# Merging triangle inverses with a transposed bracket: both factors read along a contiguous last index, three transposing copies on ScalarE per group

## The chip, the cores and the metric

One NeuronCore of a Trainium2 chip runs the whole program. The metric is device time in microseconds (us) of one execution; lower is better. The engines are called as the profile calls them: PE is TensorE (matmul), PEld its weight load, DVE is VectorE, ACT is ScalarE, POOL is GpSimd, and SP is SyncE, which here only issues DMAs.

## What is computed

The reference is a stack of two two-layer blocks in float32 on 256 tokens plus 256 context tokens. The change lies in the first layer, an RWKV-7 mixer: 32 heads of 64 channels, a recurrence over the tokens run forwards and backwards, and a readout with a normalisation per head:

```python
def step(s, inp):
    r_t, w_t, k_t, v_t, a_t, b_t = inp
    sa = jnp.einsum('bhvk,bhk->bhv', s, a_t)
    s = s * w_t[:, :, None, :] + sa[..., None] * b_t[:, :, None, :] + v_t[..., None] * k_t[:, :, None, :]
    return s, jnp.einsum('bhvk,bhk->bhv', s, r_t)
...
yn = merge_heads((y - mean) * lax.rsqrt(var + RWKV_GN_EPS))
yn = yn * p['ln_w'].astype(jnp.float32) + p['ln_b'].astype(jnp.float32)
return ((yn + merge_heads(bonus)) * jax.nn.silu(gate.astype(jnp.float32))).astype(dtype)
```

Inside a chunk of 64 tokens the term in `sa` couples every token with all earlier ones. The kernel solves that with the inverse of a triangular 64x64 matrix for each chunk, head and direction.

## The kernel before

**Stages.** After the projections of layer 0, the RWKV core works through eight groups of 256 channels (four heads each). Group g has four generators: `rwkv_prep` makes the scaled operands (AR, BK, PC), `rwkv_inverse` makes the inverses TT, `rwkv_chain` runs 16 steps (8 chunks in each of 2 directions), and `rwkv_readout` normalises and gates. `rwkv_core` (L765) interleaves them: while the chain of group g runs, the inverse of g+1, the prep of g+2 and the readout of g-1 are advanced between its steps, and so are the modulation vectors of later layers (`matvec`) and, in the last two groups, the filters of the next layer. Group 0's inverse runs earlier, beside the last projection (the gates, L702). After the core come the output product, a Hyena layer and the whole second block.

**The chain.** A step makes masked scores on PE into the PSUM tile `qk`, which DVE empties into `ATT` (L1052); then `ry` on PE, a copy to `RB` on ACT (L1083), `us` = TT times RB on PE (L1087), a copy to `UV` (L1088), the new state `st` on PE, a copy `St` on ACT (L1099), and the state update on POOL (L1101 adds, L1102 multiplies into `SB`), which the next step's `ry` of that direction reads. `qk` has two buffers, so PE stands when DVE is late with ATT.

**The inverse.** A transpose on DVE (L974) puts one 32x32 triangle on each of 128 partitions. `lane_inverse` (L1118) inverts it there. Seven small steps (L1134) invert the four 8x8 diagonal blocks. `merge8` (L1140) joins two 8x8 blocks to a 16x16 one, at rows 0 and at rows 16. `merge16` (L1154) joins those to 32x32. Each merge is two products: the bracket Z = A times X, with X the inverse of the upper block, and then the inverse of the lower block times Z. Every product is one elementwise multiply of two broadcast operands into `prod`, with index order (t, s, j) (L1131), and one sum over j (L1132). Each of merge16's two products is cut in three pieces. DVE multiplies two; POOL multiplies the third (into a tile `L`); DVE sums all three. In the layout before, the second factor is X or Z read through a rearrangement with j as its last index, so that neighbours in j lie 32, 8 or 16 floats apart. Then come two transposes (L984), copies to TT on ACT (L990), and small PE products that fill in the rest of the 64x64 inverse.

**The order.** The kernel is written against a tile framework that orders each engine's queue by playing the program through (L1917), so an edit in one place also moves other instructions. Each engine works its queue in order.

**The readout** (L1173) loads v, gate, `ln_w` (tile `rlw`) and `ln_b` (tile `rlb`) through SP's queue at its start. POOL multiplies by `rlw` (L1201) and adds `rlb` (L1202), between other steps.

## Time and profile before

| | |
|---|---|
| median of 3 runs | 2563.92 us (2564.22, 2563.92, 2555.0) |
| the profiled execution's own time | 2559.34 us |
| its span, first to last instruction | 2557.6 us |
| PE busy | 2366.6 us (93%) |
| DVE busy | 1508.1 us (59%) |
| ACT busy | 1232.6 us (48%) |
| POOL busy | 831.7 us (33%) |
[...]

The shares are averages over unlike stages, so a stage is read by itself: first how busy each engine is in it, then who ended PE's waits. A row of the views by shape gives a count, busy time in us, the mean of one in ns, the idle time before them and what ended it.

### The profile page before, as it was taken

The numbers are of one execution on the slowest core, as the hardware profiler recorded it, in microseconds if no ns is written. First come the engines' busy times: TensorE is split into PE (matmuls) and PEld (weight loads), VectorE is DVE, ScalarE is ACT, GpSimd is POOL, SyncE is SP. The second block draws the span as 40 slices with busy tenths as digits, with TensorE's granted clock in tenths as the row PEclk, the third lists the DMA queues.
The fourth block names the chain that finished last, engine by engine and source line by source line (L and its number), as shares of the span: only waits on it lengthen the run. The fifth ranks groups of instructions, "written<-read, shape, count | busy, mean of one in ns | idle before, by whom it ended". The sixth has DMA issues, their size and how long they took to land. (4 is left out here: it accounts for less than half of the span.)

```text
span 2557.6 us, 46534 instructions
## 1 busy us (share of the span) xinstructions
PE 2366.6 (93%) x19171; PEld 1992.6 (78%) x19171; DVE 1508.1 (59%) x2182; ACT 1232.6 (48%) x2270; POOL 831.7 (33%) x800
## 2 busy tenths in 40 slices
PE   6999989888887898989999999999999999999998
PEld 4578867666675676777779998788899987888886
DVE  6564495675858658665466666552435634654464
ACT  4345456665565665745344444432235623433453
POOL 4234344463545545442113332120022211121231
PEclk9999996988898988989999999999999999999999
DMA  6546442233232322204455554333222232434333
GB/s 218 201 132 204 158 141 69 85 100 107 83 113 85 120 89 79 82 21 158 149 171 173 166 169 158 115 99 99 66 85 84 65 109 83 129 124 133 108 124 132
DMA packets 203768, 306.01 MB, mean 120 GB/s; under 512 B 12593, under 2 KB 110542, under 8 KB 203556
## 3 DMA queue, kind: packets, MB, share of 16 engines
q1 hardware_dynamic: 194528, 276.08, 33.6%
q0 software_dynamic: 6096, 19.77, 2.1%
q10 hardware_dynamic: 2932, 7.18, 0.9%
q8 instruction: 151, 2.47, 0.4%
q14 instruction: 61, 0.50, 0.1%
HBM read 281.93 MB, written 21.06 MB: 118 GB/s over the span
## 5 line engine op out<-in xcount | busy, mean ns | idle before, releaser
L155 DVE TENSOR_TENSOR wlo<-wraw,whi 128x2048 fp32r<-128x2048 f32 (+1 forms) x156 | 364.5, 2338 | 310.8 <-ACT whi L154 310.6
L154 ACT CAST whi<-wraw 128x2048 fp32r<-128x2048 f32 (+1 forms) x172 | 321.9, 1875 | 296.4 <-PE x L151 153.4
L151 PE MATMUL mm<-whi,hH 128*128 128x256 f32 (+1 forms) x944 | 301.7, 322 | 4.5 <-DVE ropet L1518 1.9
L151 PE MATMUL mm<-wlo,hH 128*128 128x256 f32 (+1 forms) x944 | 300.7, 319 | 0.1
L151 PE MATMUL mm<-whi,hL 128*128 128x256 f32 (+1 forms) x944 | 299.9, 319 | 0.0
L151 PEld LDWEIGHTS mm<-whi,hH 128*128 128x128 f32 x944 | 178.5, 190 | 19.2 <-ACT rs_junk L399 2.0
L151 PEld LDWEIGHTS mm<-wlo,hH 128*128 128x128 f32 x944 | 179.0, 190 | 14.2 <-POOL wlo L155 0.3
L151 PEld LDWEIGHTS mm<-whi,hL 128*128 128x128 f32 x944 | 178.8, 190 | 14.0 <-DVE hL L355 0.2
L1052 DVE TENSOR_TENSOR ATT<-qk,mask 128x512 f32<-128x512 f32 (+1 forms) x128 | 70.6, 552 | 133.5 <-PE ry L151 86.9
L151 PE MATMUL x<-wlo,hH 128*128 128x512 f32 x352 | 140.9, 401 | 0.7 <-POOL wlo L155 0.7
L151 PE MATMUL x<-whi,hH 128*128 128x512 f32 x352 | 138.3, 399 | 1.9 <-ACT whi L154 1.9
L151 PE MATMUL ry<-UV,ATT 128*64 128x64 f32 x1536 | 139.8, 240 | 0.0
L151 PE MATMUL x<-whi,hL 128*128 128x512 f32 x352 | 139.6, 399 | 0.0
L155 POOL TENSOR_TENSOR wlo<-wraw,whi 128x2048 fp32r<-128x2048 f32 x16 | 73.6, 4598 | 201.2 <-ACT whi L154 201.2
L151 PEld LDWEIGHTS ry<-UV,ATT 128*64 128x64 f32 x1536 | 118.2, 150 | 22.2 <-issue 10.3
L1101 POOL TENSOR_TENSOR St<-St,SB 128x256 f32<-128x256 f32 x84 | 80.5, 960 | 139.0 <-ACT St L1099 131.7
L151 PE MATMUL qk<-PD,BKx 128*128 128x256 f32 x256 | 82.7, 453 | 22.4 <-DVE ATT L1052 20.9
L151 PE MATMUL us<-RB,TT 128*64 128x64 f32 x1024 | 91.1, 236 | 2.2 <-ACT RB L1083 2.0
L151 PEld LDWEIGHTS us<-RB,TT 128*64 128x64 f32 x1024 | 73.8, 145 | 21.6 <-issue 7.1
L1102 POOL TENSOR_TENSOR SB<-St,PC 128x256 f32<-128x256 f32 x98 | 81.6, 833 | 17.2 <-ACT St L1099 13.3
L1083 ACT COPY RB<-ry 64x256 f32<-64x256 f32 x128 | 46.7, 365 | 82.7 <-PE ry L151 81.0
L151 PE MATMUL us<-UV,BKt 128*128 128x128 f32 x448 | 80.5, 306 | 5.7 <-ACT UV L1088 5.6
(573 smaller groups left out, 6511.2 us busy)
## 6 DMA issues: line engine op xcount, KB each, us to landing
wraw<-in_w_in SPq DMA_DIRECT2D x68, 1024.0 KB
wraw<-in_l_w_in SPq DMA_DIRECT2D x64, 1024.0 KB
raw<-in_w_mod SPq DMA_DIRECT2D x48, 512.0 KB
wraw<-in_w_out SPq DMA_DIRECT2D x24, 1024.0 KB
raw<-in_ada_w SPq DMA_DIRECT2D x24, 512.0 KB
wraw<-in_w_branch_out SPq DMA_DIRECT2D x12, 1024.0 KB
UV<-vD SPq DMA_DIRECT2D x128, 64.0 KB
lH<-in_ada_w SPq DMA_DIRECT2D x5, 1024.0 KB
```

Of the source, the lines that this page charges most:

```text
L151: return self.nc.tensor.matmul(out, lhsT, rhs, start=start, stop=stop)
L154: self.nc.scalar.copy(hi, src)
L155: (eng or self.nc.vector).tensor_tensor(lo, src, hi.bitcast(F32), ALU.subtract)
L1052: nc.vector.tensor_tensor(at.rearrange("p i j a t -> p (i j) (a t)"), q[:, 0:256 * na].rearrange("p (h n) -> p h n", h=4), mk, ALU.mult)
L1083: nc.scalar.copy(rhs[zr], ry[0:64, 0:256])
L1101: nc.gpsimd.tensor_tensor(tmp, tmp, SB[z][step % 2], ALU.add)
L1102: nc.gpsimd.tensor_tensor(SB[z][1 - step % 2], tmp, pc, ALU.mult)
```

## The change

Four edits, three in `lane_inverse` and one in `rwkv_readout`.

1. A new tile `mW` (384 floats per partition) takes transposed copies of the upper blocks' inverses. Two copies of 8x8 (ACT, ahead of the merges) and one of 16x16 (ACT, behind `merge8(0)`) are made in each group.
2. The first product of each merge now has index order (s, t, j), from `mW` and A, so Z is stored transposed. The second product has (t, s, j) as before and reads Z as it lies. All factors have j as their contiguous last index.
3. The pieces, their sizes and their engines stay: per group four DVE multiplies of 512 elements, four of 1024, two POOL multiplies of 1024, and the same sums.
4. The readout's `ln_b` no longer has a tile of its own. It is loaded into tile `rlw` after the two multiplies by `ln_w`, and the two adds follow after a `yield`.

```diff
+        W = self.t(pool, [128, 384], "mW")
+        W8 = W[:, 0:128].rearrange("p (r a b) -> p r a b", r=2, b=8)
+        W16 = W[:, 128:384].rearrange("p (a b) -> p a b", b=16)
+        for r in range(2):
+            nc.scalar.copy(W8[:, r], X2[:, 16 * r:16 * r + 8, 16 * r:16 * r + 8].rearrange("p j s -> p s j"))
...
-            a = A2[:, r1:r1 + n, r0:r1].unsqueeze(2).to_broadcast([128, n, n, n])
-            xb = X2[:, r0:r1, r0:r1].rearrange("p s j -> p j s")
-            mulred(Z, a, xb.unsqueeze(1).to_broadcast([128, n, n, n]), (n, n, n))
+            a = A2[:, r1:r1 + n, r0:r1].unsqueeze(1).to_broadcast([128, n, n, n])
+            mulred(Z, W8[:, r0 // 16].unsqueeze(2).to_broadcast([128, n, n, n]), a, (n, n, n))
...
-            zb = Z.rearrange("p s j -> p j s")
-            mulred(X2[:, r1:r1 + n, r0:r1], a, zb.unsqueeze(1).to_broadcast([128, n, n, n]), (n, n, n))
+            mulred(X2[:, r1:r1 + n, r0:r1], a, Z.unsqueeze(1).to_broadcast([128, n, n, n]), (n, n, n))
...
+                    if n == 0:
+                        a, b = W16[:, s, j], A2[:, 16:32, 0:16][:, t, j]
+                        mulred(Z[:, s, t], a.unsqueeze(2).to_broadcast([128, ns, nt, nj]), b.unsqueeze(1).to_broadcast([128, ns, nt, nj]), (ns, nt, nj), eng)
+                    else:
+                        a, b = X2[:, 16:32, 16:32][:, t, j], Z[:, s, j]
+                        mulred(X2[:, 16:32, 0:16][:, t, s], a.unsqueeze(2).to_broadcast([128, nt, ns, nj]), b.unsqueeze(1).to_broadcast([128, nt, ns, nj]), (nt, ns, nj), eng)
...
         yield from merge8(0)
+        nc.scalar.copy(W16, X2[:, 0:16, 0:16].rearrange("p j s -> p s j"))
         yield from merge8(16)
...
-        lb = self.t(p1, [128, 256], "rlb")
-        nc.sync.dma_start(lb, I["l0_ln_b"][ch0:ch0 + 256].partition_broadcast(128))
...
             nc.gpsimd.tensor_tensor(Y[0][:, i], Y[0][:, i], lw, ALU.mult)
+        lb = self.t(p1, [128, 256], "rlw")
+        nc.sync.dma_start(lb, I["l0_ln_b"][ch0:ch0 + 256].partition_broadcast(128))
+        yield 1
+        for i in range(2):
             nc.gpsimd.tensor_tensor(Y[0][:, i], Y[0][:, i], lb, ALU.add)
-        yield 1
```

The queues differ from group 0's merges to the end of the core; ahead of that and from the output product on they read alike, but for a few rows.

DVE's queue in group 1, before, from the first bracket to the second (`prod` takes the products, `L` holds A and X, `mZ` is Z; kd, BKc, BKx and ARc belong to the prep, cols to the modulations):

```order
L1132 TENSOR_REDUCE L_3641<-prod_3714 128x4x7
L1131 TENSOR_TENSOR prod_3718<-L_3640,L_3641 128x512
L906 TENSOR_TENSOR kd_3592<-kd_3592,K_3571 128x512
L1132 TENSOR_REDUCE mZ_3717<-prod_3718 128x64
L918 TENSOR_TENSOR BKc_604_3561<-kd_3592,F_3586 128x4x64
L918 TENSOR_TENSOR BKx_605_3562<-kd_3592,F_3586 128x4x64
L923 TENSOR_TENSOR ARc_608_3565<-N_3575,P_3657 128x256
L1131 TENSOR_TENSOR prod_3772<-L_3641,mZ_3717 128x512
L1052 TENSOR_TENSOR ATT_3957<-qk_3958,mask_3278 128x512
```

The same place after the change (`mW` written by ACT):

```order
L1132 TENSOR_REDUCE L_3645<-prod_3718 128x4x7
L906 TENSOR_TENSOR kd_3596<-kd_3596,K_3575 128x512
L918 TENSOR_TENSOR BKc_605_3565<-kd_3596,F_3590 128x4x64
L918 TENSOR_TENSOR BKx_606_3566<-kd_3596,F_3590 128x4x64
L1131 TENSOR_TENSOR prod_3725<-mW_3721,L_3644 128x512
L315 TENSOR_REDUCE cols_31_133<-pp_3733 128x4
L1052 TENSOR_TENSOR ATT_3916<-qk_3917,mask_3282 128x512
```

The first bracket stood right behind the last small step; now three prep instructions lie between them, and an ATT stands close behind it.

POOL's queue at the first readout, before (`rrs` is its scale, `Y` its tile, `St` and `SB` are the chain's state):

```order
L163 TENSOR_TENSOR rrs_5130<-rstd_v_5131,mhalf_62 128x8
L886 MEMSET F_4820 128x8
L1201 TENSOR_TENSOR Y_579_3323<-Y_579_3323,rlw_4834 128x256 x2
L1101 TENSOR_TENSOR St_4938<-St_4938,SB_559_3281 128x256
L1202 TENSOR_TENSOR Y_579_3323<-Y_579_3323,rlb_4836 128x256 x2
L1102 TENSOR_TENSOR SB_558_3280<-St_4938,PC_2868 128x256
L1101 TENSOR_TENSOR St_5002<-St_5002,SB_561_3283 128x256
```

And after the change (L1208 is the multiply, L1213 the add, which now reads the reloaded `rlw`):

```order
L163 TENSOR_TENSOR rrs_5140<-rstd_v_5141,mhalf_62 128x8
L1102 TENSOR_TENSOR SB_562_3287<-St_4877,PC_2872 128x256
L1208 TENSOR_TENSOR Y_580_3327<-Y_580_3327,rlw_4842 128x256 x2
L1101 TENSOR_TENSOR St_4944<-St_4944,SB_560_3285 128x256
L1213 TENSOR_TENSOR Y_580_3327<-Y_580_3327,rlw_5274 128x256 x2
L1102 TENSOR_TENSOR SB_559_3284<-St_4944,PC_2872 128x256
```

The adds keep their place between the two halves of a state update, but what they read is now on its way from memory only from the end of the multiplies.

## Rows read from the trace of the kernel before

**Rows 1.** By stretch: length, busy us of PE, PEld, DVE, ACT, POOL, clock, DMA.
```profile
320.00:386.00 66.00, 53.05 (x256) 41.44 (x247) 64.09 (x62) 39.46 (x43) 28.50 (x32) 0.94 0.45 143
386.00:1240.00 854.00, 748.20 (x9397) 599.78 (x9394) 558.61 (x801) 506.64 (x1176) 393.02 (x421) 0.88 0.29 90
541.70:558.70 17.00, 11.87 (x100) 8.87 (x99) 16.14 (x26) 10.39 (x25) 11.94 (x11) 1.00 0.23 74
558.70:565.60 6.90, 4.54 (x20) 3.95 (x20) 6.83 (x10) 2.27 (x6) 1.52 (x4) 0.51 0.02 7
```

**Rows 2.** PE's waits, 386 to 1240 us: us in total, times, longest us.
```profile
PE qk L1057 <- DVE ATT L1052: 22.9, 12, 4.9
PE qk L151 <- DVE ATT L1052: 22.1, 8, 6.1
PE ry L151 <- POOL SB L1102: 19.3, 18, 3.2
```

**Rows 3.** DVE by shape, 320 to 1240 us: count, busy us, mean ns.
```profile
L1131 DVE TENSOR_TENSOR prod<-L,L 128x1024 f32<-128x1024 f32 x16 | 35.3, 2205 | 0.0
L1131 DVE TENSOR_TENSOR prod<-L,mZ 128x1024 f32<-128x1024 f32 x16 | 31.9, 1997 | 0.1
L155 DVE TENSOR_TENSOR wlo<-wraw,whi 128x2048 fp32r<-128x2048 f32 x10 | 22.9, 2286 | 13.9 <-ACT whi L154 13.9
L1131 DVE TENSOR_TENSOR prod<-L,mZ 128x512 f32<-128x512 f32 x16 | 21.6, 1348 | 0.2
L1131 DVE TENSOR_TENSOR prod<-L,L 128x512 f32<-128x512 f32 x16 | 20.1, 1257 | 0.3
L1199 DVE TENSOR_TENSOR Y<-Y,rrs 128x512 f32<-128x512 f32 x7 | 4.8, 691 | 8.0 <-POOL rrs L163 7.8
```

**Rows 4.** DVE's and PE's timelines, single places: start us, us, instruction, idle before it.
```profile
365.91 2.06 DVE L1131 TENSOR_TENSOR prod<-L,L 128x1024 f32<-128x1024 f32 x1
...
384.92 1.19 DVE L898 TENSOR_TENSOR_SCAN F<-keep,F 128x520 f32<-128x520 bf16 x1
...
557.04 1.59 DVE L1131 TENSOR_TENSOR prod<-L,mZ 128x512 f32<-128x512 f32 x1
...
559.38 1.03 DVE L1131 TENSOR_TENSOR prod<-L,L 128x512 f32<-128x512 f32 x1
...
561.06 1.65 PE L151 MATMUL qk<-PD,BKx 128*128 128x256 f32 x3 [6.08 <-DVE ATT L1052]
...
582.79 1.88 DVE L1131 TENSOR_TENSOR prod<-L,mZ 128x1024 f32<-128x1024 f32 x1
```

**Rows 5.** POOL by shape, 320 to 1240 us.
```profile
L1131 POOL TENSOR_TENSOR L<-L,L 128x1024 f32<-128x1024 f32 x8 | 27.4, 3427 | 2.3 <-DVE L L1132 2.3
L1201 POOL TENSOR_TENSOR Y<-Y,rlw 128x256 f32<-128x256 f32 x14 | 9.9, 728 | 5.1 <-DVE Y L1199 5.1
L1206 POOL TENSOR_TENSOR Y<-Y,rv 128x512 f32<-128x512 f32 x7 | 8.9, 1273 | 0.2
```

**Rows 6.** POOL's and DVE's timelines at one product on POOL.
```profile
569.90 2.89 POOL L1131 TENSOR_TENSOR L<-L,mZ 128x1024 f32<-128x1024 f32 x1 [2.29 <-DVE mZ L1132]
...
569.95 3.38 DVE L906 TENSOR_TENSOR kd<-kd,K 128x512 f32<-128x512 f32 x1
```

**Rows 7.** Waits of DVE, 380 to 1240 us, and one shape of ACT.
```profile
DVE L L974 <- ACT AB L965: 9.6, 5, 4.4
...
L895 ACT ACTIVATE a<-a,mhalf 128x512 f32<-128x512 f32 x28 | 20.2, 722 | 0.3
```

**Rows 8.** POOL's timeline at the first readout; last, DMAs: us to landing.
```profile
530.05 1.42 POOL L1201 TENSOR_TENSOR Y<-Y,rlw 128x256 f32<-128x256 f32 x2 [0.74 <-DVE Y L1199]
...
532.11 1.41 POOL L1202 TENSOR_TENSOR Y<-Y,rlb 128x256 f32<-128x256 f32 x2
...
gD<-ev POOLq DMA_DIRECT2D x8, 256.0 KB, 3.5
uD<-Y POOLq DMA_DIRECT2D x7, 256.0 KB, 4.3
```

## The prediction

> **What bounds the kernel now.** I read the busy times by stretch first [rows 1]. The change touches queues between 320 and 1240 us; behind that the order reads as before, so only two stretches matter. From 320 to 386 us, where group 0 is inverted, DVE is busy 64.1 of 66 us: there DVE is the bound, and what it saves should shorten the stretch one for one. From 386 to 1240 us (854 us) PE is busy 748.2, DVE 558.6, ACT 506.6 and POOL 393.0. PE bounds this stretch, but it stands idle for 854 - 748.2 = 105.8 us, and that idle time is all that a faster DVE or POOL can give back directly.

> Second, who ended PE's waits there [rows 2]: 22.9 + 22.1 = 45.0 us ended by DVE's `ATT`, 19.3 us by POOL's `SB`. So 45.0 of 105.8 us are DVE's to give back, a share of 0.43. What makes `ATT` late is to be seen in one place [rows 4]: PE starts at 561.06 after 6.08 us of waiting for it, and in DVE's queue two products of the inverse (1.59 us from 557.04, 1.03 us from 559.38) ran meanwhile. [...]

> **The change part by part.** *DVE's products.* Four of 1024 elements a group: two took 2.06 us and two 1.88 us where nothing disturbed them [rows 4]; the means are 2.21 and 2.00 us [rows 3]. What would they take with a contiguous last index? The nearest contiguous float32 rows are 0.69 us for 512 elements (L1199) and 2.29 us for 2048 (L155) [rows 3]; a straight line between them gives 0.69 + (2.29 - 0.69)/3 = 1.22 us for 1024. Savings: 2 x (2.06 - 1.22) + 2 x (1.88 - 1.22) = 3.0 us. Four of 512: the undisturbed 1.03 us [rows 4] against 0.69 saves 4 x 0.34 = 1.4 us. Together 4.4 us a group; by the means (2.21, 2.00, 1.26, 1.35 us) it would be 6.0, and zero if the contiguity of 8 or 16 floats is too short a run to count. I take 4.4, since contention has its own term below.

> [...]

> *POOL's products*, two of 1024 a group. The one at 569.90 took 2.89 us, the first kind 3.43 us on average [rows 5, 6]. Contiguous rows of POOL are 0.73 us for 256 and 1.27 us for 512 [rows 5], which carries on to 1.27 + 2 x 0.545 = 2.36 us: about 0.5 us saved each, with 1.1 us by the mean as the upper end. It counts for DVE: a two-operand instruction of DVE that started 0.05 us after POOL's took 3.38 us instead of about 0.7 [rows 3, 6], so it ends when POOL ends. DVE gains 2 x 0.5 = 1.0 us a group. Relief of DVE in all: 5.4 us a group.

> [...]

> *The three copies on ACT.* ACT's row for 128x512 is 0.72 us [rows 7]; the copies have 64 or 256 elements, so 0.72 x 3 = 2.2 us a group is the upper end, 17 us on an engine busy 506.6 of 854 us. ACT does not bound the stretch, and I put 1 us on the path (bounds 0 and, by 2.2 us in each group, 17).

> *The handoff.* DVE's first bracket now waits for ACT's copy, behind whatever ACT is doing; an `ATT` stands two rows behind it on DVE and would wait with it. As cover, three prep instructions now lie between the last small step and that bracket. When DVE waits for ACT in the transpose at L974 today it costs 9.6 / 5 = 1.9 us, 4.4 at most [rows 7]. So 0 to 4.4 us a group; with the cover I take 1.0, in group 0 too. POOL's first product also waits for the 16x16 copy, with `SB` behind it, but DVE's two pieces of it are no earlier, so nothing is counted.

> *Group 0:* relief -5.4, handoff +1.0; and DVE's scan L898 (1.19 us [rows 4]), which ran behind group 0's inverse, now comes ahead of its last transposes: +1.2. Sum -3.2 us, one for one.

> *Groups 1 to 7:* 7 x (5.4 - 1.0) = 30.8 us less of DVE. How much reaches PE? All of it would if every such product stood ahead of an `ATT` for which PE waits; the share of PE's idle time ended by `ATT` is 0.43. The products lie closer to these stalls than DVE's average instruction, so I take half: -15.5 us (bounds 0 and -31).

> *The readout.* Before, `ln_b` lay in its own tile and POOL's adds ran from 532.11, 0.64 us behind the multiplies' end at 530.05 + 1.42 = 531.47 [rows 8]. Now the load can only be issued at that end. Loads of the readout's size land 3.5 to 4.3 us after issue [rows 8], so the adds start at about 535.0 to 535.8 instead of 532.1: 2.9 to 3.7 us later, and `SB` (L1102) of one direction stands behind them on POOL, for which PE's `ry` waits. In four of six readouts beside the chain POOL's order leaves that `SB` behind the adds; in two it has moved ahead. I take 3.2 x 4/6 = 2.2 us for each, 13 us; half of it reaches PE, since the other direction's work is in between: +6.5 us (bounds 0 and 28, that is six times 4.3 and the issue). The last two readouts end long before they are needed.

> *Clock.* PE's mean of 0.88 in the core [rows 1] is a mixture of the two levels in which 0.12 x 748 = 90 us of full-speed work is lost at most. The idle time given back so far, 15.5 - 6.5 - 1 = 8 of 105.8 us, would bring 90 x 8 / 105.8 = 6.8 us if all slow stretches followed stalls; I take half, -3.4.

> *Sum:* -3.2 - 15.5 + 6.5 + 1.0 - 3.4 = -14.6 us. The profiled execution took 2559.3 us, so the forecast is **2545 us**. The median of the three runs, 2563.9, lies 4.6 us above that execution, and one run was at 2555.0; the forecast stands against the profiled one.

> **The rivals.**

> *B, the relief stops at DVE.* `ATT` moves together with the products: DVE's new order puts one right behind the first bracket, which waits for ACT. If that gives back what the shorter products win, groups 1 to 7 bring nothing, and -3.2 + 6.5 + 1.0 = +4.3 gives about 2564. For it: DVE idles 295 of 854 us, so it has time to lose already. Against it: its idle time is not where PE waits.

> *C, slower: the readout's load decides.* If POOL stands for 4.7 us in each of six readouts and all of it reaches PE through `SB`, the chain is last in those groups and DVE's relief shows in one group of seven: -3.2 - 2.2 + 28 + 1 = +24, about 2583. It is slower than before once a readout costs PE more than (3.2 + 15.5 - 1) / 6 = 3.0 us. For it: `SB` already ends 19.3 us of PE's waits [rows 2]. Against it: the longest of them is 3.2 us, and two of six places are reordered.

> *D, the relief arrives whole* and the readout is hidden: -3.2 - 31 + 1 = -33, with the clock (90 x 30 / 105.8 / 2 = 13) up to -46: about 2520. For it: DVE is busy 16.14 of 17 and 6.83 of 6.9 us in the merges [rows 1], so queues there are never empty.

> *E, the change does not do what it says.* If the price of the layout is that of four-dimensional broadcast patterns and not of the stride, nothing is saved; copies, handoffs and the readout are added: +1.0 + 1.2 + 7 x 1.0 / 2 + 6.5 + 1.0 = +13, about 2573. [...] Against it, by the rows: `Y` with a broadcast `rrs` (L1199) is a three-dimensional pattern with a broadcast operand and takes 0.69 us, the products of the same size 1.03 and more [rows 3, 4].

> **How the numbers follow.** Chances: forecast A 0.44, B 0.20, C 0.14, D 0.15, E 0.07. A measurement of this kernel can tell about 0.5% from no change, 12.8 us; against the profiled execution that puts the bounds at 2546.5 and 2572.1. A lies close to the lower one and spreads by about 12 us: 0.26 faster, 0.18 same. D is faster (0.15), B same but for 0.03 on the fast side and 0.02 on the slow one, C slower but for 0.02, E half and half. Faster 0.44, same 0.38, slower 0.18. The range runs from 2520, in the middle of D, to 2576, and leaves out half of D and most of C, some 0.18. The likeliest case by itself would be 2533 to 2557.

> **What would show it.** DVE's products near 1.22 us (1024) and 0.69 us (512), POOL's near 2.4 us; if they stay at 2 and 1 us, E holds. PE's waits ended by `ATT` down from 45.0 us by a third; if they are not, B holds, and DVE's waits for `mW` should name the reason. PE's waits ended by `SB` up from 19.3 us by less than 10; if by 20 or more, with POOL's adds waiting for a DMA, C holds. The first stretch should end about 3 us earlier. The forecast fails above all if the share of DVE's relief that reaches PE is far from a half.

## The result and the profile after

| | before | after |
|---|---|---|
| median | 2563.92 us (5 runs, 2555.0 to 2566.2) | **2503.21 us** (5 runs, 2494.3 to 2506.1) |
| ratio | | 0.9774, 95% interval 0.9755 to 0.9792 |
| profiled execution's span | 2557.6 us | 2501.4 us |
| mean granted TensorE clock | 0.948 | 0.964 |
| PE busy | 2366.6 us | 2341.5 us |
| DVE, POOL busy | 1508.1, 831.7 us | 1461.9, 813.0 us |

By the ratio the kernel is faster by 58 us, by the medians by 61. The forecast was 2545 us, 15 us faster, with a range from 2520 to 2576: the direction is right, the time lies outside the range. A second session beside other runs of the kernel before gave the changed kernel 2503.03 us and 0.9782 (0.9759 to 0.9805).

The gain lies where the change is. The core ends at 1185 us instead of 1238; behind it the two kernels differ by 3 us (1316 us after, 1320 before). By stretch (length, busy us of PE, PEld, DVE, ACT, POOL, clock, DMA share, GB/s), to be read against [rows 1]:

```profile
320.00:386.00 66.00, 52.05 (x296) 40.71 (x295) 56.22 (x63) 44.33 (x50) 25.61 (x25) 0.93 0.47 156
386.00:1185.00 799.00, 725.25 (x9396) 580.40 (x9394) 521.14 (x798) 509.08 (x1191) 375.64 (x427) 0.92 0.31 95
```

PE's idle time in the core is 799 - 725.3 = 73.7 us, after 105.8. And PE is busy for 23 us less with the same work, at a granted clock of 0.92 instead of 0.88. So of the 55 us by which this stretch is shorter 32 are waiting, and 23, two fifths, are speed. What ended PE's waits (us in all, times, longest), to be read against [rows 2]:

```profile
PE ry L151 <- POOL SB L1102: 21.3, 18, 2.7
...
PE qk L1057 <- DVE ATT L1052: 6.2, 6, 2.0
PE qk L151 <- DVE ATT L1052: 5.8, 7, 1.9
```

The waits for `ATT` fell from 45.0 to 12.0 us, and the longest from 6.1 to 2.0. `SB` ends 21.3 us, hardly more than the 19.3 of before. The products themselves, by shape (count, busy us, mean ns, idle before), DVE's ahead and POOL's behind, against [rows 3, 5]:

```profile
L1131 DVE TENSOR_TENSOR prod<-mW,L 128x1024 f32<-128x1024 f32 x16 | 27.4, 1710 | 0.0
L1131 DVE TENSOR_TENSOR prod<-L,mZ 128x1024 f32<-128x1024 f32 x16 | 20.0, 1247 | 0.1
...
L1131 DVE TENSOR_TENSOR prod<-L,mZ 128x512 f32<-128x512 f32 x16 | 16.9, 1054 | 0.2
L1131 DVE TENSOR_TENSOR prod<-mW,L 128x512 f32<-128x512 f32 x16 | 14.0, 877 | 1.1 <-ACT mW L1145 0.8
...
L1131 POOL TENSOR_TENSOR L<-L,mZ 128x1024 f32<-128x1024 f32 x8 | 23.9, 2992 | 7.0 <-DVE mZ L1132 7.0
L1131 POOL TENSOR_TENSOR L<-mW,L 128x1024 f32<-128x1024 f32 x8 | 21.0, 2630 | 6.4 <-ACT mW L1178 6.3
```

The four DVE groups together took 108.9 us and take 78.3. The means still hold the time in which POOL's products block them (one of 1024, from 865.98 us, took 3.35 us while a product of POOL ran for 2.77 us from 865.48); single undisturbed ones are at 1.21 and 0.67 us (1024 elements at 360.78, 512 at 350.21), POOL's shortest at 2.34 us. That is what was forecast: 1.22, 0.69 and 2.36.

### The profile page after: what moved, and what is told of

It is laid out like the page before. It is cut to its first block, busy times and chain, and to the rows that moved or that the text cites. A ratio compares the mean times of both kernels' runs of the same rounds, so it can differ in the third digit from the quotient of the medians.

```text
span 2501.4 us, 46570 instructions
## 1 busy us (share of the span) xinstructions
PE 2341.5 (94%) x19171; PEld 1971.5 (79%) x19171; DVE 1461.9 (58%) x2182; ACT 1239.3 (50%) x2294; POOL 813.0 (32%) x800
## 5 line engine op out<-in xcount | busy, mean ns | idle before, releaser
L155 DVE TENSOR_TENSOR wlo<-wraw,whi 128x2048 fp32r<-128x2048 f32 (+1 forms) x156 | 367.1, 2355 | 317.4 <-ACT whi L154 317.2
L155 POOL TENSOR_TENSOR wlo<-wraw,whi 128x2048 fp32r<-128x2048 f32 x16 | 73.6, 4599 | 201.1 <-ACT whi L154 201.1
L1101 POOL TENSOR_TENSOR St<-St,SB 128x256 f32<-128x256 f32 x84 | 73.1, 870 | 126.7 <-ACT St L1099 97.2
L1102 POOL TENSOR_TENSOR SB<-St,PC 128x256 f32<-128x256 f32 x98 | 77.9, 795 | 24.5 <-ACT St L1099 19.5
L151 PE MATMUL qk<-PD,BKx 128*128 128x256 f32 x256 | 75.7, 421 | 7.2 <-DVE ATT L1052 5.4
```

What stands on the lines that cost most here:

```text
L151: return self.nc.tensor.matmul(out, lhsT, rhs, start=start, stop=stop)
L155: (eng or self.nc.vector).tensor_tensor(lo, src, hi.bitcast(F32), ALU.subtract)
L1101: nc.gpsimd.tensor_tensor(tmp, tmp, SB[z][step % 2], ALU.add)
L1102: nc.gpsimd.tensor_tensor(SB[z][1 - step % 2], tmp, pc, ALU.mult)
```

## The experiments

| kernel | time | at the lower level | difference | of it clock | rest |
|---|---|---|---|---|---|
| changed kernel | 2503.2 | 180 | -53 | -28 | -25 |
| f1 contiguous, order of before | 2512.1 | 206 | -45 | -19 | -25 |
| f3 the same, DVE's products only | 2525.8 | 222 | -31 | -14 | -17 |
| f4 the same, POOL's only | 2556.2 | 261 | 0 | 0 | 0 |
| f2 strided, order of after | 2536.5 | 200 | -20 | -21 | +1 |
| e3 readout alone | 2562.4 | 251 | +6 | -3 | +9 |
| e1 contiguous, scheduled anew | 2498.7 | 192 | -58 | -24 | -34 |
| c1 copies on DVE | 2510.4 | 201 | -46 | -21 | -25 |
| v1 all pieces on DVE | 2514.5 | 236 | -42 | -9 | -33 |
| g1 before, stalls filled | 2536.6 | 178 | -20 | -29 | +9 |
| g2 after, stalls filled | 2497.9 | 150 | -59 | -39 | -20 |
| v2 v1, stalls filled | 2508.7 | 206 | -48 | -19 | -29 |

**Length of the products or order of the queues?** The scheduler prices the access pattern, so a new pattern also gives a new order. Two kernels change one of the two alone. They are scheduled as the kernel before, or as the changed one, and the patterns are exchanged afterwards in the finished program, so that every engine's queue stays as it was row for row (in the traces DVE's 2185 instructions and POOL's 807 stand in the same order). For f1:

```diff
+    for blk in nc.m.functions[0].blocks:
+        blk.instructions = [_reread(i) if i.opcode == "TensorTensor" and i.debug.lineno == 1131 else i for i in blk.instructions]
```

where `_reread` swaps the last two dimensions of the factor whose last step is not 1. f2 does the reverse to the factors from `mW` and `mZ`.

> The kernel before in its own order, every engine's queue row for row, no copies and no change of the readout; only the second factor of the merges' products (DVE's 64 and POOL's 16) is read with a step of 1 in the finished program (the elements come in another order, so the inverses' values are not those of the reference). Theory 'duration' (the shorter products take DVE out of PE's way): PE's waits ended by ATT fall from 45.0 to under 20 us, the time by 30 to 55 us, to 2507 to 2535. Rival 'order' (the gain comes from the places that the scheduler gave the products and the work around them): at most a third of the 58 us, 2545 to 2564.

> The changed kernel in its own order, row for row, with its copies and its readout; only the factors from mW and mZ are read with a step of 8 or 16 floats again in the finished program (values not those of the reference). 'Duration': the products are back at 1.9 to 2.2 us (1024) and 1.0 to 1.4 us (512), the ATT waits are back above 35 us, and the time is 2550 to 2575. 'Order': the time stays within 20 us of the changed kernel, 2503 to 2523, though the products are as long as before.

Measured: f1 2512.08 us, ratio 0.9827 (0.9783 to 0.9872); f2 2536.51 us, 0.9935 (0.9907 to 0.9963). Shorter products alone bring about three quarters of the gain; the order alone brings about a third; the two overlap a little. Put the other way round, shorter products bring 45 us in the old order and 33 us (2536.5 to 2503.2) in the new one. Both theories named a part, the first the larger one: f1's time lies in the range of 'duration', but its waits for `ATT` did not fall below the 20 us that it expected, and f2's time lies between the two ranges. The core of f1 by stretch, PE's waits, and DVE's products of 1024:

```profile
386.00:1192.00 806.00, 726.93 (x9326) 583.08 (x9327) 516.06 (x798) 500.72 (x1165) 365.68 (x417) 0.90 0.30 93
...
PE qk L1057 <- DVE ATT L1052: 17.1, 11, 3.6
PE qk L151 <- DVE ATT L1052: 16.4, 8, 4.1
PE ry L151 <- POOL SB L1102: 8.9, 12, 2.4
...
L1131 DVE TENSOR_TENSOR prod<-L,L 128x1024 f32<-128x1024 f32 x16 | 23.8, 1488 | 0.0
L1131 DVE TENSOR_TENSOR prod<-L,mZ 128x1024 f32<-128x1024 f32 x16 | 19.8, 1238 | 0.1
```

and PE's waits and the products of 1024 in f2, which are as long as before or longer:

```profile
PE ry L151 <- POOL SB L1102: 25.5, 22, 3.6
PE qk L151 <- DVE ATT L1052: 14.2, 12, 3.8
PE qk L1057 <- DVE ATT L1052: 10.4, 8, 3.1
...
L1131 DVE TENSOR_TENSOR prod<-mW,L 128x1024 f32<-128x1024 f32 x16 | 39.4, 2462 | 0.0
L1131 DVE TENSOR_TENSOR prod<-L,mZ 128x1024 f32<-128x1024 f32 x16 | 31.2, 1948 | 0.1
```

With the order kept, shorter products do not remove the waits for `ATT` (45.0 to 33.5 us); almost as much comes back through `SB` (19.3 to 8.9 us). Which engine's products bring that, f3 and f4 below tell. With the length kept, the new order takes `ATT` from 45.0 to 24.6 us, and the longest wait from 6.1 to 3.8. Only together do they reach 12.0.

The experiments e1, e3, c1 and v1 below are scheduled anew, and their queues differ from those of the kernel that they are held against. A new order alone was worth 20 us in f2, so a difference of that size in them can't be put down to the edit by itself.

**Without the additions.** e1 leaves the rearrangements out, so that the products read contiguously with no copy and no change of the readout, and lets the scheduler order it anew. As in f1 to f4 one factor's elements come in another order, so it computes other inverses than the reference's.

```diff
-            xb = X2[:, r0:r1, r0:r1].rearrange("p s j -> p j s")
+            xb = X2[:, r0:r1, r0:r1]
...
-            zb = Z.rearrange("p j s -> p s j")
+            zb = Z
```

> The kernel before with the rearrangements of X and Z simply left out, so that the products read contiguously without any copy (they then multiply by the transposed factor, values not those of the reference); the readout as before; the scheduler orders it anew. 'Duration': as the changed kernel or a little better, 2490 to 2515, since the copies on ACT, DVE's wait for them and the readout's late load are not there. 'Order': anything from 2500 to 2564, since this order is neither of the two.

Measured: 2498.75 us, 0.9775 (0.9717 to 0.9834), the ratio of the changed kernel. So the copies, the handoffs and the late load together cost nothing that this measurement sees, each kernel in the order that it was given. By the estimate of the rest it would be 9 us (-34 against -25). The changed kernel without its fourth edit was not run.

**The readout alone**, the fourth edit on the kernel before:

```diff
-        lb = self.t(p1, [128, 256], "rlb")
-        nc.sync.dma_start(lb, I["l0_ln_b"][ch0:ch0 + 256].partition_broadcast(128))
...
             nc.gpsimd.tensor_tensor(Y[0][:, i], Y[0][:, i], lw, ALU.mult)
+        lb = self.t(p1, [128, 256], "rlw")
+        nc.sync.dma_start(lb, I["l0_ln_b"][ch0:ch0 + 256].partition_broadcast(128))
+        yield 1
+        for i in range(2):
             nc.gpsimd.tensor_tensor(Y[0][:, i], Y[0][:, i], lb, ALU.add)
-        yield 1
```

> The kernel before with the fourth edit alone: ln_b loaded into rlw after the multiplies, the adds behind a yield. As the prediction put it: +13 us of POOL's time and +6.5 on the end, 2570 (bounds 2564 and 2592). If the scheduler's new places for the readout bring something by themselves: 2545 or less.

Measured: 2562.43 us, 1.0022 (0.9996 to 1.0048). The core by stretch, POOL's waits for the load, and PE's for `SB` behind them:

```profile
386.00:1242.00 856.00, 739.56 (x9398) 592.22 (x9399) 553.55 (x800) 506.64 (x1175) 390.94 (x420) 0.90 0.29 89
...
POOL Y L1204 <- DMA rlw<-in_l_ln_b: 17.9, 7, 3.8
...
PE ry L151 <- POOL SB L1102: 30.8, 25, 3.2
```

The term fits: 17.9 us on POOL (13 forecast for six readouts), 30.8 - 19.3 = 11.5 us on PE's waits, and 6 us on the end (6.5 forecast; by the interval -1 to +12, so no change is not excluded, and the new order is in it). In the changed kernel POOL waits for the load almost as long, but the waits ended by `SB` are only 2 us up on before. Shorter products make up for a part: f2, with the same order and the same late load but long products, has 25.5 us of them, 4 more. The other 5 us lie between e3 and f2, which have different orders; what in the order does it stays open.

```profile
POOL Y L1213 <- DMA rlw<-in_l_ln_b: 14.4, 7, 3.3
```

**DVE's products or POOL's?** f3 and f4 are f1 restricted to one engine.

> As f1_contig_order_before (order of the kernel before, row for row), but only DVE's 64 products read with a step of 1; POOL's 16 stay strided. If the gain of 44 us comes from DVE's own products (108.9 us of them in all became 73.3 there), this run keeps three quarters of it: 2518 to 2532. If POOL's shorter hold on DVE and SB's earlier turn are the larger part, it keeps less than half: 2535 to 2550.

> The counterpart: only POOL's 16 products read with a step of 1, at 2.7 us instead of 3.3. POOL is free 10 us sooner in all, and DVE, which stands behind each of them with one instruction, as well. First theory: 2543 to 2555. Second theory (POOL's hold is the larger part): 2525 to 2540, with PE's waits ended by SB down from 19.3 to about 9 us as in f1_contig_order_before.

Measured: f3 2525.77 us, 0.9876 (0.9843 to 0.9910); f4 2556.22 us, 0.9989 (0.9967 to 1.0010). DVE's own products carry the larger part, 31 of f1's 45 us. POOL's, by themselves, became shorter (2.90 and 2.72 us instead of 3.43 and 3.23 on average) and brought nothing measurable; whether they add to DVE's is open, since the intervals of f1 and f3 overlap. PE's waits and POOL's two instructions of the state update, first in the kernel before:

```profile
L1102 POOL TENSOR_TENSOR SB<-St,PC 128x256 f32<-128x256 f32 x98 | 81.6, 833 | 17.2 <-ACT St L1099 13.3
L1101 POOL TENSOR_TENSOR St<-St,SB 128x256 f32<-128x256 f32 x84 | 80.5, 960 | 139.0 <-ACT St L1099 131.7 <-PE ry L151 7.2
```

in f3:

```profile
PE qk L151 <- DVE ATT L1052: 22.0, 7, 5.0
PE qk L1057 <- DVE ATT L1052: 18.5, 11, 4.1
PE ry L151 <- POOL SB L1102: 10.9, 14, 2.3
...
L1102 POOL TENSOR_TENSOR SB<-St,PC 128x256 f32<-128x256 f32 x98 | 74.1, 758 | 16.6 <-ACT St L1099 12.8
L1101 POOL TENSOR_TENSOR St<-St,SB 128x256 f32<-128x256 f32 x84 | 73.9, 882 | 136.2 <-ACT St L1099 121.6 <-PE ry L151 7.9 <-PE us L151 6.2
```

and in f4:

```profile
PE ry L151 <- POOL SB L1102: 22.4, 20, 3.2
...
L1101 POOL TENSOR_TENSOR St<-St,SB 128x256 f32<-128x256 f32 x84 | 85.4, 1018 | 131.5 <-ACT St L1099 122.8 <-PE ry L151 8.7
L1102 POOL TENSOR_TENSOR SB<-St,PC 128x256 f32<-128x256 f32 x98 | 78.4, 801 | 15.9 <-ACT St L1099 12.0
```

So it is DVE's shorter products, and not POOL's, that take the waits for `SB` down (10.9 us in f3, 22.4 in f4, against 19.3). With them POOL's state updates themselves take 148.0 us instead of 162.1 (147.1 in f1), and 163.8 in f4. The prediction counted only that POOL's products hold DVE. That DVE's products hold POOL in the same way is the likely reading of these rows; no run tries it by itself. The waits for `ATT` fell by only 4.5 us in f3.

**The copies on DVE.** `nc.scalar.copy` becomes `nc.vector.tensor_copy` in the two lines that make a group's three copies.

> The changed kernel with its three copies a group on DVE instead of ACT: no wait of DVE or POOL for ACT, but 24 short instructions more on DVE, at an estimated 0.2 to 0.5 us (5 to 12 us in all). If the handoff to ACT costs what the prediction put on it (1 us a group, half on the end), the two cancel: 2495 to 2512. If the handoff is free and every us of DVE reaches the end, 2508 to 2516.

Measured: 2510.39 us, 0.9809 (0.9775 to 0.9842). It can't be told from the changed kernel, and it lies in both of the ranges that were expected, so it doesn't decide between them. On DVE the copies took 0.37 and 0.44 us on average, 8.8 us in all, where 5 to 12 were estimated. The trace of the changed kernel is more direct: of all handoffs DVE waited for one, POOL for three.

```profile
DVE prod L1131 <- ACT mW L1145: 0.8, 1, 0.8
...
POOL L L1131 <- ACT mW L1178: 6.3, 3, 2.7
```

**Is the clock a cause, or a companion?** g1 is the kernel before with nothing shortened. At the 32 instructions at which PE stood longest in the trace, extra matmuls of a constant are put in front, sized to the stall, into PSUM banks which no engine uses at that point; nothing else in any queue changes.

```diff
+FILL = {'pi<-fw,hdn': {2: (3, 'ry_2324_12229')},
...
+ 'qk<-PD,BKx': {4: (8, 'ry_719_3969'), 22: (15, 'us_961_5224'), 36: (11, 'ry_1204_6466'), 52: (13, 'us_1435_7681'), 80: (3, 'us_1889_10067')},
...
+            for _ in range(count):
...
+                out.insert(at, mybir.InstMatmult(name=f"I-{n}", engine=i.engine, debug=i.debug, ins=s, outs=[o], start_tensor_calc=True,
+                                                 stop_tensor_calc=True, tile_size=like.tile_size, tile_position=like.tile_position))
```

> The kernel before, every queue in its own order, with nothing shortened; only PE gets 174 extra matmuls (128x128, of a constant, into PSUM banks that nobody uses then), 59 us of work at full clock, put in front of the 32 instructions at which PE stood for 1.2 us or more between 400 and 1237 us (75.5 us of idle time in all). If the time at the lower clock follows PE's stalls and costs what the repeated runs of one kernel show (about 0.4 us for each us at the lower level; 261 us in the median of before), filling them brings 60 to 110 us less of it and 2515 to 2540. If the clock is only a companion of the stalls, the extra matmuls are hidden at best: 2555 to 2600.

Measured: 2536.57 us, 0.9932 (0.9909 to 0.9956). More work for PE, and the kernel is faster by 0.7%. The time at the lower level fell from 261 to 178 us. In the trace (of an execution of 2546.4 us, 10 us above the median) the extra matmuls take 48 us in all, not the 59 that were expected, and the stall of 6.08 us from [rows 4] now holds 15 extra matmuls (x30, two records each), and the stretch around it runs at 1.00 where [rows 1] shows 0.51 behind the stall. PE's timeline, the stretch (the columns of [rows 1]), and PE's waits:

```profile
547.86 3.62 PE L151 MATMUL us<-ident 128*128 128x128 f32 x30
551.45 0.92 PE L151 MATMUL qk<-PD,BKx 128*128 128x256 f32 x3
...
544.00:561.00 17.00, 14.84 (x140) 12.03 (x140) 16.90 (x23) 9.54 (x23) 10.71 (x12) 1.00 0.21 69
...
PE qk L1057 <- DVE ATT L1052: 12.9, 12, 2.0
PE ry L151 <- POOL SB L1102: 10.7, 13, 1.6
PE qk L151 <- DVE ATT L1052: 8.2, 9, 2.4
```

The queues and the work of DVE, ACT and POOL are as before, so PE's clock is a cause and no mere companion. It is not the whole of the gain: with nearly the same time at the lower level as the changed kernel (178 against 180 us), g1 is 33 us slower.

**A version that beats both?** The same fill was tried on the changed kernel (g2). v1 puts the third piece of merge16's products on DVE too (`eng = nc.vector`), because DVE stood behind POOL's products for some 28 us (in the trace of the changed kernel DVE's instructions that ran beside them are by so much longer in all than the shortest of their kind). v2 is v1 with its stalls filled.

> The same with the changed kernel: 85 extra matmuls (29 us at full clock) in front of the 19 instructions at which PE stood for 1.2 us or more in its own trace (38.6 us in all). If the clock follows the stalls, 40 to 80 us less at the lower level (180 in the median) and 2475 to 2495, faster than both kernels. If it is only a companion: 2503 to 2525.

> The changed kernel with the third piece of both products of merge16 on DVE as well. DVE gains 16 products of 1.21 us (+19 us) and loses the 28 us for which it now stands behind POOL's products; POOL loses 45 us, and SB has no product in front of it. If every us of DVE reaches the end, as in f1_contig_order_before, about 9 us less, and some us less of SB's waits: 2485 to 2500. If POOL's products were hidden, 19 us more: 2515 to 2525.

> v1_all_on_dve with 59 extra matmuls (20 us at full clock) in front of the 15 instructions at which PE stood for 1.2 us or more in its trace (26.1 us in all). v1 had the fewest waits of all kernels so far but 236 us at the lower level in its median. If its disadvantage against the changed kernel is the clock, and the clock follows the stalls, 40 to 60 us less at the lower level: 2490 to 2505. If its stretches at the lower level come from sparse work of PE and not from stalls, as the trace suggests for four of them, the fill brings little: 2508 to 2520.

> The changed kernel once more, beside the same runs of the kernel before as v2_all_on_dve_filled: 2495 to 2510, at 165 to 195 us at the lower level. It is the yardstick for g2_fill_after, v1 and v2, and it says how far a second chip session repeats the ratio of 0.977.

Measured: g2 2497.85 us, 0.9772 (0.9743 to 0.9802); v1 2514.51, 0.9826 (0.9796 to 0.9857); v2 2508.68, 0.9797 (0.9773 to 0.9821); the changed kernel again 2503.03, 0.9782 (0.9759 to 0.9805). None beats it by more than the interval. g2 has 150 us at the lower level, 30 less than the changed kernel where 40 to 80 less were expected, and its time lies between the two ranges. v1 shows why the waits are not enough to look at: PE waits less for `ATT` than in the changed kernel, yet its core runs at 0.89 and its median has 236 us at the lower level. By stretch (the whole core, and 10 us of it), and PE's waits for `ATT`:

```profile
386.00:1196.00 810.00, 741.47 (x9385) 593.97 (x9386) 508.04 (x811) 508.60 (x1189) 339.40 (x412) 0.89 0.30 93
...
500.60:510.80 10.20, 10.20 (x108) 8.31 (x110) 4.08 (x8) 4.87 (x13) 3.10 (x4) 0.50 0.20 66
...
PE qk L1057 <- DVE ATT L1052: 6.7, 8, 1.9
PE qk L151 <- DVE ATT L1052: 3.6, 7, 1.3
```

From 500.6 to 510.8 PE is busy for all of the 10.2 us and is granted 0.50 the whole time; in the 15 us before, at 1.00, its longest wait was 0.41 us. Not every stretch at the lower level comes from a stall, and filling v1's stalls brought 30 us less at the lower level and 6 us of time, which is within the intervals. What sends PE there while it is busy stays open.

## Why the forecast was wrong

**The lengths were right.** 1.22, 0.69 and 2.36 us were forecast; 1.21, 0.67 and, for POOL's two kinds at their shortest, 2.34 and 2.37 were measured. A straight line between contiguous rows of the same engine was enough. The step in the last index has a price of its own here: f1 exchanges nothing but the step, and products of 1024 go from 2.21 and 2.00 to 1.49 and 1.24 us on average. Rival E is out with it.

**Half of DVE's relief reaching PE was right, as long as the clock is left out.** By the prediction's own terms f1, which has no copies and no late load, is -5.4 for group 0 and -37.8 / 2 = -18.9 for the others, -24; the estimate of the rest is -25. f1's trace agrees: in the core PE is idle for 105.8 - 79.1 = 27 us less and DVE busy for 42 us less. In the changed kernel it is 32 of 38 us, but there the new order has its part in it. That the size fits is in part luck, because the way there was only partly the one described: the prediction had the relief come through `ATT`, and in f1 as much came through `SB`, by way of POOL's state updates, for which the sum had nothing. POOL's own share, a fifth of the relief in the sum and so some 4 us on the end, lies within f4's interval and is neither shown nor excluded.

**The additions were put at +13; together with the new order they cost about nothing.** With half of the handoffs (3.5 for groups 1 to 7, 2.2 in group 0 with the scan), 6.5 for the readout and 1 for the copies, the sum of -24 became -11. The changed kernel's rest is -25, that of f1. Of this the readout's term fits in the kernel before (e3) but is for the most part covered in the changed one, where `SB` lost 2 us instead of 11. Its landing times were read from stores of 256 KB on POOL's queue, while the load has 128 KB and goes through SP's; by luck they served (in e3 POOL waited 2.6 us on average, 3.8 at most). The handoff was mis-sized: 1.0 us a group forecast, 0.8 us in all measured on DVE, and 6.3 us on POOL, for which the sum had nothing. In group 0, where -3.2 us was forecast one for one, almost nothing came: DVE was busy for 7.9 us less, but `us` of group 0 starts at 408.1 instead of 408.6 us, while it starts at 404.4 in f1 in the old order. There the new order spent the gain (the scan L898 ahead of the transposes, and 2.3 us of waiting for POOL).

**The step that failed is the clock.** It stood in the sum with -3.4 us, as half of the share of 90 us that the net idle time given back (8 of 105.8 us) would bring. By the estimate it was -28 (-17 to -44), and in the traces PE is busy for 23 us less in the core. Both inputs were too small. The idle time given back was 32 us and not 8: the readout's +6.5 and the copies' +1 were subtracted and did not show, and the relief itself brought more than 15.5. And no row spoke for taking half. With 32 us and no halving the prediction's own rule gives 90 x 32 / 105.8 = 27 us. That does not prove the rule: v1 gives 37 us of idle time back, for which it would be 32 us, and PE is busy there for 7 us less; e3 has 11 us more of idle time, and PE is busy for 9 us less. What g1 shows is that long stalls carry much of the loss: with 32 of them filled, the time at the lower level fell by 83 us. Rival D, whose -31 for the whole relief is near to the 32 us, would have ended at 2500 with 90 x 30 / 105.8 = 26 us of clock instead of the half that was taken there; it had a chance of 0.15.

**The order was not in the sum at all.** f2, with products as long as before, is 20 us faster than before, all of it by the estimate from the clock (261 to 200 us at the lower level): the new places break up the longest waits without shortening DVE's work (the longest for `ATT` is 3.8 us instead of 6.1). The prediction used the moved rows as cover for the handoff, as a cost in group 0 and as a danger (rival B), never as a gain. The sign of such a move could not be read from the queues; its size, 0.65% by the ratio, is as large as the forecast's whole gain.

**Why the range missed.** Rivals and bounds were made from waits, with at most 13 us of clock (rival D). That the clock could be worth more was to be seen: 90 us of lost work were counted, and the three runs at hand spread by 9 us with the same program (the 55 later ones by 25). The clock term had no bounds of its own; 0 to -30 would have covered the estimate.

## What to carry to other kernels

A float32 product on DVE with a step of 8, 16 or 32 floats in its last index costs 1.5 to 1.7 times the contiguous one here (1.88 and 2.06 against 1.21 us, 1.03 against 0.67), and a transposing copy of 64 to 256 elements on an engine with time to spare (0.30 and 0.65 us on ACT) pays for it. When an edit shortens work in front of a PE that runs at a mixed clock, give the clock a term and a range of its own: look for the long single waits that go, since idle time in all did not set it in v1 and e3, and price it from repeated runs of one kernel (time against granted clock). Look in both directions when two engines hold each other: here POOL's state updates took 162.1 us before and 148.0 us with shorter products on DVE alone (f3), probably because DVE's products hold POOL too. To separate an edit from the order that a scheduler makes of it, exchange the operands in the finished program, both ways.

## What the runs showed of the hardware that was not expected

A us at the lower level costs this kernel an estimated 0.35 us. That is less than PE's own work lagged behind the stall of 6.08 us: the three matmuls of `qk` there took 1.65 us [rows 4], and 0.92 us at 1.00 in g1, an estimated 0.44 us of each. Giving PE 48 us of needless work made the kernel 20 us faster (g1, 0.9932), with 83 us less at the lower level. POOL's state updates took 162.1 us before and 148.0 us when only DVE's products were made shorter (f3). And in v1 PE was granted 0.50 for 10.2 us in which it is busy throughout by the records.
